# Neighbourhood attention in a hybrid encoder layer: the keys' copies to the other partitions issued by GpSimd in place of SyncE

## The chip, the core and the metric

The kernel runs on one core of a Trainium2 chip. The core has TensorE (PE) for matmuls, VectorE (DVE), ScalarE (ACT) and GpSimd (POOL) for element work, and SyncE (SP), which here does nothing but issue transfers. The transfers themselves are carried by 16 DMA engines that all issuers share. The metric is the time of one launch on the device in microseconds (us). Engines run their own instructions in order and wait for one another through semaphores.

## What is computed

The reference is one layer of an encoder on 512 positions of 1024 channels, in float32: a token mixer, a cross-attention into 256 memory tokens and a gated MLP. The mixer projects the normed input once and feeds three branches, a long convolution (Hyena), a neighbourhood attention and a short gated convolution, whose results are gated and merged. The change lies in the neighbourhood attention. The 512 positions form a grid of 8 rows by 64 columns; each position attends, in each of 8 heads of 64 channels, to all 8 rows and to 16 columns around its own:

```python
s = jnp.einsum('bhrqd,bhrkcd->bhrqkc', qg, k_rows).astype(jnp.float32)
s = s + bias[None].astype(jnp.float32)
s = jnp.where(col_mask[:, None, :], s, -1e30)
p = jax.nn.softmax(s, axis=(-2, -1)).astype(v.dtype)
o = jnp.einsum('bhrqkc,bhrkcd->bhrqd', p, v_rows)
```

## The kernel before

**Split products.** A matmul of the precision needed is made of three: every float32 operand is split into a high part in a shorter format (`high`, ACT, L76) and the remainder (`low`, DVE, L79), and `mm3` (L89 to L91) adds high by high, low by high and high by low in PSUM. A projection (`project`) is eight times `mm3` over tiles of 128 by 512.

**Heads.** The attention works on pairs of heads. `na_project` makes q and k of one pair, 128 channels, by two projections; a head owns 64 of the 128 partitions (`own`), the other half is `oth`. For the scores of a head, q and k are packed so that two matmuls do what three do elsewhere: the tile qa holds the high part of q in `own` and its low part in `oth`; ka holds k's high part in `own` and its low part in `oth`; kb holds the same two parts with the halves exchanged. Then qa by ka (L705) and qa by kb (L706) together give all four products of the parts. A low part is written by DVE straight into the other half of the partitions; the exchange for kb is made by two transfers inside the core, 64 partitions of 512 numbers each (128 KB), the first of the high part (L681), the second of the low part (L682). The second can start only when DVE has written ka's low half. There are 16 such transfers, two for each of 8 heads. kb has three buffers.

**Weights.** `na_weights` (a step: one head and half of its 4 column blocks) needs the bias tiles gm of the head: a transfer on SP loads rpb (L693), and POOL adds the mask to it in three additions (L697), into four buffers that DVE frees when it has added them to the scores (L712). Then softmax. The first step also loads the value tiles v, eight transfers of 256 KB issued by SP (L629).

**What runs beside.** `natten` goes through 19 steps; the four pairs are projected at steps 0, 2, 6 and 10, and a pair that is projected at one of the last three is first used two steps later. In each step one piece of other work is laid between, from a generator (`merge_first`: projections for the merge gates, branch products, and two additions of 128 by 512 on POOL, L803). Their weights are loaded by SP (`load_raw`, L120). Elsewhere POOL also issues transfers: accumulating weight loads before this stage (L106), and loads and stores of factor sums in the MLP (L1096, L1101).

**Order.** The program is written through a layer that derives all semaphores and plans each engine's order when the kernel is built: it takes the instructions by their place in the text, but lets a later one go ahead where the earlier one is not ready by its own reckoning of times. An engine's order is therefore not the text's order, and it is fixed when the kernel runs.

Of the kernel before, what the change touches and what calls it, by code (L numbers as in the profile page):

```python
# [34 lines left out]
def f(ap):  # L35
    return ap.bitcast(F32)
# [10 lines left out]
def shaped(ap, offset, *dims):  # L47

    return bass.AP(ap.tensor, ap.offset + offset, [list(ap.ap[0])] + [list(q) for q in dims])


class Trunk:
# [611 lines left out]
    def na_project(self, pool, hp, x):  # L664

        nc, d = self.nc, self.d
        pq = self.project(d["w_in"][12 + hp], x)
        pk = self.project(d["w_in"][16 + hp], x)
        out = []
        for e in range(2):  # L670
            own, oth = slice(64 * e, 64 * e + 64), slice(64 - 64 * e, 128 - 64 * e)
            qa = pool.tile([P, L], F32R, tag="qa", bufs=4, name="qa")
            src = shaped(pq[own, :], 7 * 64 + 15, [16, 4], [-64, 8], [-1, 16])
            self.high(qa[own, :].rearrange("p (b r c) -> p b r c", b=4, r=8), src)
            self.low(qa[oth, :].rearrange("p (b r c) -> p b r c", b=4, r=8), src,
                     qa[own, :].rearrange("p (b r c) -> p b r c", b=4, r=8))
            ka = pool.tile([P, L], F32R, tag="ka", bufs=4, name="ka")
            kb = pool.tile([P, L], F32R, tag="kb", bufs=3, name="kb")
            self.high(ka[own, :], pk[own, :])
            self.low(ka[oth, :], pk[own, :], ka[own, :])  # L680
            nc.sync.dma_start(out=f(kb[oth, :]), in_=f(ka[own, :]))  # L681
            nc.sync.dma_start(out=f(kb[own, :]), in_=f(ka[oth, :]))  # L682
            out.append([qa, ka, kb, None])
        return out

# [798 lines left out]
```

## Time and profile before

| | us |
|---|---|
| median of three runs | 1085.06 |
| the three runs | 1084.93, 1085.06, 1089.47 |
| the profiled execution | 1087.84 |
| its span, first to last instruction | 1086.1 |
| PE busy in the span | 1056.7 (97%) |
| DVE, ACT, POOL busy | 746.7, 520.1, 101.4 |
| mean granted clock of PE | 0.99 |

The profile is one execution, recorded by the hardware. Its views are a page of totals; waits, that is, who stood idle until whom; the chain of work that ended last, followed backwards; groups of instructions by source line and tile; instructions in order of time; and busy times in chosen stretches, with the granted clock of PE. A tile is named by the program's name. The neighbourhood attention lies between about 240 and 390 us.

### The profile page before, as it was taken

Reading aid. Unit: us, or ns where it says so; the run is one execution under the profiler, and the core shown is the slowest. Engines: PE = TensorE matmul, PEld = TensorE weight load, DVE = VectorE, ACT = ScalarE, POOL = GpSimd, SP = SyncE. Lnnn points to the kernel's source line nnn. Section 1 sums busy time; section 2 is a strip of 40 time slices with the busy share of each in tenths; the row PEclk is TensorE's granted clock in tenths of the full one; section 3 lists DMA queues with packets and bytes.
Section 4 is the critical chain, followed back from the end, with each engine's and each line's share of the span. In section 5 each row is a group of like instructions: output and inputs, shape, how many; then the busy total and the mean of one; then the engine's idle time right before and its main releaser. Section 6 shows DMA issues by size and latency. Waiting matters only on the chain.

```text
span 1086.1 us, 13877 instructions
## 1 busy us (share of the span) xinstructions
PE 1056.7 (97%) x5166; PEld 883.6 (81%) x5166; DVE 746.7 (69%) x1182; ACT 520.1 (48%) x817; POOL 101.4 (9%) x120
## 2 busy tenths in 40 slices
PE   9989999999999999999999999999997999999996
PEld 6768888887888888888798888898886888888885
DVE  7986498874674763436796455579867776667687
ACT  6756554345557642324564444345332434346464
POOL 1061410001120100000000000001211000000000
PEclk9989999999999999999999999999998999999999
DMA  6597986527333322226245321247888333226663
GB/s 226 170 263 204 286 201 159 131 80 181 120 105 94 109 72 97 97 97 232 98 148 195 124 78 43 75 137 271 298 284 275 131 99 112 96 83 193 193 195 126
DMA packets 60400, 167.71 MB, mean 154 GB/s; under 512 B 6473, under 2 KB 13321, under 8 KB 60332
## 3 DMA queue, kind: packets, MB, share of 16 engines
q1 hardware_dynamic: 51116, 133.27, 37.5%
q0 software_dynamic: 9216, 33.56, 11.7%
q8 instruction: 40, 0.66, 0.2%
q14 instruction: 28, 0.23, 0.1%
HBM read 145.83 MB, written 18.87 MB: 152 GB/s over the span
## 4 chain that ended last, share of the span: by engine, by line
PE 76%; DMA 9%; DVE 8%; issue 4%; ACT 2%; POOL 0%; SPq 0%; DVEq 0%; POOLq 0%; ACTq 0%
PE mm L90 23%; PE mm L89 23%; PE mm L91 22%; DMA sums<-sum 4%; DMA sum<-in_ffn_down 2%; PE aux L90 2%; PE aux L89 2%; PE aux L91 2%; DVE wl L79 1%; PE aux L736 1%; PE aux L725 1%; DMA raw<-in_hy_o 1%; DMA nc_raw<-in_xt 1%; DVE hf L431 1%; DMA wr<-in_w_out 0%
## 5 line engine op out<-in xcount | busy, mean ns | idle before, releaser
L79 DVE TENSOR_TENSOR wl<-wr,wh 128x1024 fp32r<-128x1024 f32 (+2 forms) x173 | 209.0, 1210 | 155.9 <-ACT wh L76 155.0
L76 ACT ACTIVATE wh<-wr 128x1024 fp32r<-128x1024 f32 (+3 forms) x193 | 198.2, 1027 | 243.3 <-PE mm L90 174.7
L89 PE MATMUL mm<-hh,wh 128*128 128x512 f32 (+1 forms) x448 | 168.4, 377 | 6.6 <-DVE u L341 6.3
L90 PE MATMUL mm<-hl,wh 128*128 128x512 f32 (+1 forms) x448 | 168.5, 376 | 1.2 <-DVE hl L79 1.2
L91 PE MATMUL mm<-hh,wl 128*128 128x512 f32 (+1 forms) x448 | 168.2, 376 | 0.0
L89 PE MATMUL mm<-xh,wh 128*128 128x512 f32 x416 | 165.0, 397 | 0.0
L90 PE MATMUL mm<-xl,wh 128*128 128x512 f32 x416 | 163.6, 393 | 0.0
L91 PE MATMUL mm<-xh,wl 128*128 128x512 f32 x416 | 163.4, 393 | 0.0
L89 PEld LDWEIGHTS mm<-hh,wh 128*128 128x128 f32 x448 | 84.7, 190 | 22.7 <-issue 7.1
L90 PEld LDWEIGHTS mm<-hl,wh 128*128 128x128 f32 x448 | 84.9, 190 | 16.3 <-DVE hl L79 1.4
L91 PEld LDWEIGHTS mm<-hh,wl 128*128 128x128 f32 x448 | 84.9, 190 | 15.1
L91 PEld LDWEIGHTS mm<-xh,wl 128*128 128x128 f32 x416 | 78.8, 189 | 16.7
L90 PEld LDWEIGHTS mm<-xl,wh 128*128 128x128 f32 x416 | 79.1, 190 | 16.0 <-issue 0.3
L89 PEld LDWEIGHTS mm<-xh,wh 128*128 128x128 f32 x416 | 78.9, 190 | 16.1 <-issue 0.3
L1099 DVE TENSOR_TENSOR sum<-sum 128x512 f32<-128x512 f32 x44 | 30.2, 689 | 24.6 <-DMA sum<-in_ffn_down 24.3
L89 PE MATMUL mm<-wh,sh 128*128 128x512 f32 x110 | 42.8, 389 | 0.0
L91 PE MATMUL mm<-wh,sl 128*128 128x512 f32 x110 | 42.8, 389 | 0.0
L90 PE MATMUL mm<-wl,sh 128*128 128x512 f32 x110 | 42.8, 389 | 0.0
L1035 ACT ACTIVATE u<-u 128x512 f32<-128x512 f32 x22 | 13.9, 632 | 55.2 <-DVE u L341 55.2
L1096 POOL DMA_DIRECT2D sum<-in_ffn_down x22 | 11.8, 536 | 289.2 <-DVE nt L895 234.4
L341 DVE SCALAR_TENSOR_TENSOR u<-mm,cols,u 128x511 f32<-128x511 f32 x44 | 33.0, 749 | 1.0
L333 DVE SCALAR_TENSOR_TENSOR u<-mm,cols,u 128x511 f32<-128x511 f32 x44 | 32.8, 745 | 0.2 <-ACT u L332 0.2
(367 smaller groups left out, 2098.7 us busy)
## 6 DMA issues: line engine op xcount, KB each, us to landing
wr<-in_w_in SPq DMA_DIRECT2D x53, 512.0 KB, 3.5
wr<-in_ffn_up SPq DMA_DIRECT2D x44, 512.0 KB, 4.1
sum<-in_ffn_down POOLq DMA_DIRECT2D x22, 512.0 KB, 4.7
sums<-sum POOLq DMA_DIRECT2D x22, 512.0 KB, 6.2
wl<-in_w_in POOLq DMA_DIRECT2D x20, 512.0 KB, 6.7
wr<-sums SPq DMA_DIRECT2D x20, 512.0 KB, 4.2
wr<-in_ffn_down SPq DMA_DIRECT2D x15, 512.0 KB, 3.5
wr<-in_w_branch SPq DMA_DIRECT2D x12, 512.0 KB, 3.5
```

The lines of the kernel that those rows point to most:

```text
L76: self.nc.scalar.activation(out=out, in_=in_, func=ACT.Copy, bias=0.0, scale=scale)
L79: (eng or self.nc.vector).tensor_tensor(out=out, in0=in_, in1=f(high), op=ALU.subtract)
L89: mm(out, ah, bh, start=first, stop=False)
L90: mm(out, ah, bl, start=False, stop=False)
L91: mm(out, al, bh, start=False, stop=last)
L333: nc.vector.scalar_tensor_tensor(out=out[:, 1:L], in0=ps[:, 0 : L - 1], scalar=self.colvec(w0), in1=out[:, 1:L], op0=ALU.mult, op1=ALU.add)
L341: nc.vector.scalar_tensor_tensor(out=out[:, 0 : L - 1], in0=ps[:, 1:L], scalar=self.colvec(w2), in1=out[:, 0 : L - 1], op0=ALU.mult, op1=A ...
L431: nc.vector.tensor_tensor(out=s, in0=s, in1=part[1][0:1, :], op=ALU.add)
L725: nc.tensor.transpose(tr[:, i * P : (i + 1) * P], s[:, i // 2, (i % 2) * P : (i % 2 + 1) * P], self.ident[:])
L1035: nc.scalar.activation(out=u[:], in_=u[:], func=ACT.Gelu_apprx_tanh)
L1096: nc.gpsimd.dma_start(out=t[:], in_=w[k, i])
L1099: v.tensor_tensor(out=out, in0=x, in1=y, op=ALU.subtract)
```

## The change

The two transfers that fill kb are issued by GpSimd and no longer by SyncE; their data, sizes and dependencies stay as they are.

```diff
             self.high(ka[own, :], pk[own, :])
             self.low(ka[oth, :], pk[own, :], ka[own, :])
-            nc.sync.dma_start(out=f(kb[oth, :]), in_=f(ka[own, :]))
-            nc.sync.dma_start(out=f(kb[own, :]), in_=f(ka[oth, :]))
+            nc.gpsimd.dma_start(out=f(kb[oth, :]), in_=f(ka[own, :]))
+            nc.gpsimd.dma_start(out=f(kb[own, :]), in_=f(ka[oth, :]))
             out.append([qa, ka, kb, None])
         return out
```

## The prediction

> **What bounds the kernel now.** I read the page's busy times first, then TensorE's waits over the whole span, then the chain of waits around the one wait that names the edited tile.
>
> ```profile
> span 1086.1 us, 13877 instructions
> PE 1056.7 (97%) x5166; PEld 883.6 (81%) x5166; DVE 746.7 (69%) x1182; ACT 520.1 (48%) x817; POOL 101.4 (9%) x120
> PE mm L89 <- DVE u L341: 6.3, 2, 6.0
> PE aux L423 <- DVE hf L426: 4.7, 1, 4.7
> PE aux L706 <- DMA kb<-ka: 2.4, 1, 2.4
> PE aux L90 <- DVE sl L79: 1.4, 1, 1.4
> ```
>
> TensorE (PE) sets the time: it is busy for 1056.7 of 1086.1 us, so 29.4 us in all can be won by waiting less. GpSimd (POOL) is nearly idle. The edit can reach PE only through the tile kb, and PE waited for kb once, for 2.4 us (the columns of a wait are total us, times, longest). The chain of waits and PE's instructions in order of time show where:
>
> ```profile
> 251.66 0.69 DVE ka L79
> 252.38 5.30 DMA kb<-ka
> 257.81 0.36 PE aux L706
> ...
> 252.06 0.39 PE L89 MATMUL mm<-xh,wh 128*128 128x512 f32 x1
> 252.40 0.39 PE L705 MATMUL aux<-ka,qa 128*128 128x256 f32 x1
> 252.63 0.39 PE L90 MATMUL mm<-xl,wh 128*128 128x512 f32 x1
> ...
> 255.12 0.28 PE L705 MATMUL aux<-ka,qa 128*128 128x256 f32 x1
> 257.81 0.36 PE L706 MATMUL aux<-kb,qa 128*128 128x256 f32 x1 [2.41 <-DMA kb<-ka]
> ```
>
> This is the first head of the first pair. The second copy of its kb is issued at 252.38, as soon as the low part is written, and lands 5.30 us later at 257.68; PE is free at 255.12 + 0.28 = 255.40 and stands until 257.81. It also shows that PE's order isn't the order of the text: L705 stands among the matmuls of another product, and its partner L706 comes eleven matmuls later. The order is planned when the kernel is built, and a planner that is told of another queue may plan it anew.
>
> The gap is followed by a slow stretch. The columns that matter in the next rows are the stretch, then, after the engines' busy times, the granted clock, the DMA share and GB/s:
>
> ```profile
> 249.00:251.00 2.00, 2.00 (x11) 1.65 (x10) 0.59 (x1) 1.65 (x2) 0.50 (x1) 1.00 1.07 249
> 258.00:259.00 1.00, 1.00 (x7) 0.87 (x7) 0.47 (x1) 0.98 (x2) 0.00 (x0) 0.97 1.06 173
> 259.00:260.00 1.00, 1.00 (x5) 0.80 (x3) 1.00 (x3) 0.45 (x1) 0.00 (x0) 0.50 1.07 198
> 260.00:262.00 2.00, 2.00 (x7) 1.71 (x7) 1.39 (x2) 0.57 (x3) 0.74 (x2) 0.50 0.98 272
> 262.00:264.00 2.00, 2.00 (x9) 1.60 (x9) 1.88 (x4) 0.52 (x3) 1.43 (x2) 0.91 0.81 324
> ```
>
> At half clock PE is "busy" but loses 0.03 + 0.50 + 2 x 0.50 + 2 x 0.09 = 1.71 us of full-speed work. So the one wait costs 2.41 + 1.71 = 4.12 us, and that is the most the edit can win at this place. The shares near 1.0 also say that all DMA engines are saturated there, which is why a copy took 5.3 us.
>
> **The change part by part.** Sixteen copies (two a head) leave SP's queue and enter POOL's. What SP had around the first four, and what the copies cost where nothing else moves:
>
> ```profile
> 251.02 0.52 SPq L681 DMA_DIRECT2D kb<-ka  x1
> 251.59 0.59 SPq L629 DMA_DIRECT2D v<-vd  x1
> 252.38 0.49 SPq L682 DMA_DIRECT2D kb<-ka  x1
> 253.00 0.51 SPq L681 DMA_DIRECT2D kb<-ka  x1
> 253.73 0.46 SPq L682 DMA_DIRECT2D kb<-ka  x1
> 254.28 0.65 SPq L693 DMA_DIRECT2D rpb<-in_na_rpb  x1
> 254.99 0.98 SPq L120 DMA_DIRECT2D wr<-in_w_in  x2
> ...
> kb<-ka SPq DMA_DIRECT2D x4, 128.0 KB, 2.3
> ...
> sum<-in_ffn_down POOLq DMA_DIRECT2D x22, 512.0 KB, 4.7
> wr<-in_ffn_down SPq DMA_DIRECT2D x15, 512.0 KB, 3.5
> ...
> L1096 POOL DMA_DIRECT2D sum<-in_ffn_down x22: 527/532/594, 723.2 to 825.3; - x22
> ```
>
> *Issue.* POOL takes a median of 532 ns for one plain transfer, so sixteen add 16 x 0.53 = 8.5 us to its 101.4; it has the room, and SP gets back about as much (16 x 0.5). The POOL price is measured on 128-partition loads from memory, not on 64-partition copies inside the core; I take it as it is, the copies having fewer rows.
>
> *Landing.* The four copies of the second pair, with the DMA engines less full, landed after 2.3 us, against 5.3 in the first pair: 3.0 us of the first was waiting, behind the value loads (L629) that stand before it in the same queue and beside them on the engines. No row shows this copy issued by POOL. Its bounds: from below 2.3 us, the copy unhindered with POOL no slower than SP; from above 5.3 + 1.2 = 6.5, all the waiting kept, plus the 4.7 - 3.5 = 1.2 us by which POOL's loads of the same matrix landed later than SP's. I take 2.3 + 1.2 for the path, and for the saturated engines the copy's own share counted twice: 128 KB at 249 GB/s is 0.5 us, and shared half and half with SP's transfers it takes 0.5 longer. Together 4.0 us, nearer the lower end, because a copy in POOL's own queue has nothing ahead of it there.
>
> The Trainium skill, DMA: Bandwidth & Descriptors, in its section on SWDGE, HWDGE and iDMA, says that the two kinds of queue are separate inside each DMA engine, which takes them in turn; by that the waiting behind the value loads goes and the sum is the one below. The same page's section "Issuing engines are not separate DMA queues" says that issuing from another engine only saves the issuer's time; by that the 3.0 us stays, which is my first rival. No row of before decides between them.
>
> *The sum.* Landing at 252.38 + 4.0 = 256.38, plus the 0.13 us that passed before from landing to matmul, gives 256.51; PE, free at 255.40, stands 1.1 us in place of 2.41 and wins 1.3. Will the clock still fall? The longest wait that left it whole is this one:
>
> ```profile
> 149.90 0.39 PE L90 MATMUL aux<-sl,wavefh 128*128 128x256 f32 x1 [1.40 <-DVE sl L79]
> ...
> 146.00:150.00 4.00, 2.60 (x13) 1.94 (x11) 4.00 (x8) 3.52 (x4) 1.68 (x2) 1.00 0.76 306
> 150.00:154.00 4.00, 4.00 (x29) 3.78 (x30) 3.97 (x6) 3.71 (x6) 1.28 (x2) 1.00 0.73 124
> ```
>
> After a wait of 1.40 us the clock stayed at 1.00, after 2.41 it halved. A gap of 1.1 lies below the first, so I count the 1.7 us as won: 1.3 + 1.7 = 3.0 us. If PE's order is planned with the copy a little later, other matmuls fill the gap and the win rises towards 4.1; I take no such shift, the lower bound of it. Worth zero is the later end: landing at 6.5 us makes the gap 258.88 + 0.13 - 255.40 = 3.6, a loss of 1.2 and, if the slow stretch doubles, of 2.9.
>
> The Trainium skill, TensorE: Matmul & The Clock Gate, under "Why this matters for your kernels", asks that gaps stay below about 3 us to keep the clock. Here 2.41 us was enough to halve it, so the trace is stricter than the page; by the page's figure the clock would owe nothing to the gap and the win would be 1.3 alone (1083.8).
>
> *The later pairs.* Three more pairs of heads issue four copies each, now behind POOL's additions to the bias tiles (L697), which wait for VectorE:
>
> ```profile
> 280.23 0.50 SPq L682 DMA_DIRECT2D kb<-ka  x1
> 282.80 0.47 SPq L682 DMA_DIRECT2D kb<-ka  x1
> ...
> 278.42 1.44 POOL L697 TENSOR_TENSOR gm<-rpb,mask 128x256 f32<-128x256 f32 x2 [14.95 <-DVE nas L712]
> 285.46 0.74 POOL L697 TENSOR_TENSOR gm<-rpb,mask 128x256 f32<-128x256 f32 x1 [5.61 <-DVE nas L712]
> 289.70 0.76 POOL L697 TENSOR_TENSOR gm<-rpb,mask 128x256 f32<-128x256 f32 x1 [3.49 <-DVE nas L754]
> ...
> 291.11 0.28 PE L706 MATMUL aux<-kb,qa 128*128 128x256 f32 x1
> ```
>
> The second pair's first head needs its kb at 291.11. Issued at 280.23 it lands by 280.23 + 4.0 = 284.2, almost 7 us early; POOL stood idle for 5.61 us before 285.46, room for four issues of 0.53. Even behind the addition at 285.46 (over at 286.20) two issues and 4.0 us end at 291.3, about on time. So I cost the moved queue at nothing, hidden under the matmuls between L681 and L706. In the other direction, additions that come behind copies start up to 2.1 us later, and POOL's own idle time ahead of them (5.61 and 3.49 us) takes that up. SP's loads behind the copies, first the rpb at 254.28 and the weights at 254.99, may go some 2 to 4 us earlier (SP was held from 251.02 on); PE is full there and waits for none of them, so this is worth nothing, though it puts 1 MB more beside the first copies.
>
> The profiled execution took 1087.84 us, 1.74 more than its span and 2.8 more than the median, 1085.06, of the three runs. The sum is made on its stretches and taken off the median: 1085.06 - 3.0 = 1082.0 us.
>
> **The rivals.**
> *No queue of its own* (slower than before). The copies wait on the saturated engines as before and come by POOL's longer path: 6.5 us, gap 3.6. For it: DMA shares of 1.07 on all engines, and the weights that SP now issues earlier. Against it: SP's queue demonstrably held the value load of 251.59 ahead of the copy. It decides as soon as POOL's copy takes over 5.3 us. Time 1085.06 + 1.2 = 1086.3.
> *Caught behind the additions* (slower). If the order on POOL puts a pair's copies behind the addition of 289.70 (over at 290.46), two issues and 4.0 us make 295.5, 4.4 us after 291.11, and 1.7 of slow clock follows: 6.1 us for a pair, 1091.2; 18 for all three, 1103. It decides once copies are issued after about 286. For it: POOL works its queue in order and the additions wait up to 5.6 us; against it: at 280 to 283 POOL stood idle.
> *A new order elsewhere.* The planner moves matmuls or loads beyond this stage. The largest stall is 6.0 us (L89 behind L341); one more such costs 6 before any clock loss and gives 1082.0 + 6 = 1088 or worse, one less 1076. Nothing in the rows says that the order far from the copies should move.
> *Nothing moves*: the copy lands within half a microsecond of 5.3 and the clock falls as before, 1085.
>
> **How the numbers follow.** Forecast, win of 1.3 to 4.1 us: 0.50. No queue of its own: 0.17; nothing moves: 0.08. Caught behind the additions: 0.11. New order: worse 0.09, better 0.05. What a measurement can tell from no change, 0.5%, is 5.4 us, so faster means under 1079.6 and slower over 1090.5. Faster comes from the better new order and a little of the forecast's edge: 0.08. Slower comes from the caught copies and half of the worse order: 0.15. Same: 0.77. The range goes from 1079.5, just beyond the full 4.1 with 1.5 for the spread of the runs, to 1088.5, past the first rival's 2.9 us; left out are the caught copies and the ends of the new order, about 0.2.
>
> **What would show it.** Right: PE's wait at the first L706 is about 1 us or gone, the clock from 258 to 264 stays at 1.00, the first pair's kb lands within about 4 us of its issue, L681 and L682 stand on POOL at some 0.53 us each, no later L706 waits for kb. Wrong: a first landing over 5.3 us, a PE wait for kb in a later pair, POOL issuing those copies after 286, or a new wait of PE over 2 us elsewhere.

## The result, and the profile after

The change made the kernel slower: 1091.45 us against 1085.44 us, medians of 22 runs each, a ratio of 1.0053 with a 95% interval of 1.0039 to 1.0068. That is half a percent, some 5.8 us by the ratio (the medians lie 6.0 apart), where I had forecast 3.0 less.

The page of the changed kernel, and PE's waits over the span (total us, times, longest):

```profile
span 1090.2 us, 13892 instructions
PE 1058.4 (97%) x5166; PEld 885.0 (81%) x5166; DVE 747.3 (69%) x1182; ACT 520.2 (48%) x817; POOL 109.6 (10%) x136
```

```profile
PE aux L706 <- DMA kb<-ka: 5.4, 1, 5.4
PE aux L423 <- DVE hf L426: 4.7, 1, 4.7
PE mm L89 <- DVE u L341: 3.6, 1, 3.6
```

There is still one wait for kb, at the same place, and it grew from 2.4 to 5.4 us. The stage's chain of waits in order of time says why:

```profile
253.41 0.70 DVE ka L79
254.11 0.29 issue
254.40 7.90 DMA kb<-ka
262.30 0.14 issue
262.44 0.55 PE aux L706
```

The second copy, issued by POOL 0.3 us after ka's low half was written, took 7.90 us to land, not 5.30 as before and not 4.0 as I had it. (The whole picture lies 1.75 us later than in the profile of before; that was there ahead of the stage, where the two programs are the same.) SP's queue ahead of the copies, in order of time (start, duration of the issue or of the run of issues), in the kernel before and then in the changed one:

```profile
243.01 4.42 SPq L629 DMA_DIRECT2D v<-vd  x7
251.02 0.52 SPq L681 DMA_DIRECT2D kb<-ka  x1
```

```profile
244.74 5.06 SPq L629 DMA_DIRECT2D v<-vd  x8
250.05 0.62 SPq L693 DMA_DIRECT2D rpb<-in_na_rpb  x1
250.77 2.98 SPq L120 DMA_DIRECT2D wr<-in_w_in  x2
```

Before, rpb and the two weight loads stood behind the four copies, at 254.28 and 254.99. SP had been held by the copies, which waited for ka, ever since the seventh value load was out at 243.01 + 4.42 = 247.43, and not only from 251.02 on, as the prediction has it. Now SP is free: it issues them from 250.05 on, ahead of the copies. That is 192 + 2 x 512 = 1216 KB more on engines that were full before; at the 249 GB/s of before I estimate it at 5.0 us of transfer. The copy did not pay all of that: it landed 2.6 us later than in the profile of before, where the same loads came behind it but were in flight with it. The clock's stretch behind the gap grew with it (the granted clock is the number before the last two):

```profile
260.00:261.00 1.00, 0.00 (x0) 0.00 (x0) 0.00 (x0) 1.00 (x1) 0.00 (x0) 0.61 1.18 188
261.00:262.00 1.00, 0.00 (x0) 0.00 (x0) 0.00 (x0) 0.23 (x1) 0.00 (x0) 0.50 0.62 127
262.00:263.00 1.00, 0.56 (x2) 0.59 (x3) 0.00 (x0) 0.00 (x0) 0.00 (x0) 0.50 0.51 164
263.00:264.00 1.00, 1.00 (x5) 0.90 (x5) 0.47 (x1) 0.00 (x0) 0.00 (x0) 0.50 0.09 33
264.00:266.00 2.00, 2.00 (x8) 1.61 (x7) 2.00 (x4) 0.00 (x0) 0.73 (x1) 0.50 0.00 0
266.00:268.00 2.00, 2.00 (x9) 1.63 (x9) 1.97 (x5) 1.09 (x4) 0.74 (x1) 0.74 0.46 106
```

From PE's restart on, 0.28 + 0.50 + 1.00 + 0.52 = 2.3 us of full-speed work are lost. Gap and clock cost 5.4 + 2.3 = 7.7 us here, against 4.1 in the profile of before. The later pairs cost nothing, as forecast; the second pair's copies on POOL, in order of time:

```profile
283.68 0.74 POOL L697 TENSOR_TENSOR gm<-rpb,mask 128x256 f32<-128x256 f32 x1 [15.72 <-DVE nas L712]
284.36 0.52 POOL L681 DMA_DIRECT2D kb<-ka  x1
284.89 0.76 POOL L697 TENSOR_TENSOR gm<-rpb,mask 128x256 f32<-128x256 f32 x1
285.75 0.53 POOL L682 DMA_DIRECT2D kb<-ka  x1
286.38 0.52 POOL L681 DMA_DIRECT2D kb<-ka  x1
288.33 0.52 POOL L682 DMA_DIRECT2D kb<-ka  x1 [1.43 <-DVE ka L79]
```

They slipped in among the additions, and the transfers of that stretch landed 2.2 us after issue:

```profile
kb<-ka POOLq DMA_DIRECT2D x4, 128.0 KB, 2.2
```

### The profile page after: what moved, and what is told of

The parts are those of the page before. It is cut to its first block, busy times and chain, and to the rows that moved or that the text cites. A ratio compares the mean times of both kernels' runs of the same rounds, so it can differ in the third digit from the quotient of the medians.

```text
span 1090.2 us, 13892 instructions
## 1 busy us (share of the span) xinstructions
PE 1058.4 (97%) x5166; PEld 885.0 (81%) x5166; DVE 747.3 (69%) x1182; ACT 520.2 (48%) x817; POOL 109.6 (10%) x136
## 4 chain that ended last, share of the span: by engine, by line
PE 76%; DMA 8%; DVE 8%; issue 4%; ACT 2%; POOL 1%; SPq 0%; DVEq 0%; POOLq 0%; ACTq 0%
PE mm L89 23%; PE mm L90 23%; PE mm L91 23%; DMA sums<-sum 3%; DMA sum<-in_ffn_down 2%; PE aux L90 1%; PE aux L89 1%; PE aux L91 1%; DVE wl L79 1%; PE aux L736 1%; DMA kb<-ka 1%; PE aux L725 1%; DMA raw<-in_hy_o 1%; DMA nc_raw<-in_xt 1%; POOL sum L1096 1%
## 5 line engine op out<-in xcount | busy, mean ns | idle before, releaser
L89 PE MATMUL mm<-hh,wh 128*128 128x512 f32 (+1 forms) x448 | 169.0, 378 | 3.9 <-DVE u L341 3.6
L89 PE MATMUL mm<-xh,wh 128*128 128x512 f32 x416 | 165.2, 397 | 0.0
L89 PEld LDWEIGHTS mm<-hh,wh 128*128 128x128 f32 x448 | 85.5, 191 | 19.6 <-issue 4.0
L89 PEld LDWEIGHTS mm<-xh,wh 128*128 128x128 f32 x416 | 79.0, 190 | 16.0 <-issue 0.3
L89 PE MATMUL mm<-wh,sh 128*128 128x512 f32 x110 | 42.8, 389 | 0.0
L341 DVE SCALAR_TENSOR_TENSOR u<-mm,cols,u 128x511 f32<-128x511 f32 x44 | 32.9, 748 | 0.9
L712 DVE SCALAR_TENSOR_TENSOR nas<-aux,gm 128x256 f32<-128x256 f32 x32 | 18.1, 608 | 21.7 <-PE aux L706 19.9
```

The source lines that it names most:

```text
L89: mm(out, ah, bh, start=first, stop=False)
L341: nc.vector.scalar_tensor_tensor(out=out[:, 0 : L - 1], in0=ps[:, 1:L], scalar=self.colvec(w2), in1=out[:, 0 : L - 1], op0=ALU.mult, op1=A ...
L712: nc.vector.scalar_tensor_tensor(out=s[:, i, :].rearrange("p (c r) -> p c r", r=8), in0=shaped(ps[:], i * 256, *turned), scalar=0.125, in1 ...
```

## The experiments

Two theories stood after this. **A, the loads let go:** moving the copies frees SP, whose loads get in front of them, and the copies wait for that traffic, whoever issues them. **B, POOL's queue:** a copy issued by POOL is served slower beside SP's queue. Line numbers stay those of the kernel before.

**Only the first pair on POOL, only the later pairs on POOL.** Which copies carry the loss? In the first kernel:

```diff
-            nc.sync.dma_start(out=f(kb[oth, :]), in_=f(ka[own, :]))
+            (nc.sync if hp else nc.gpsimd).dma_start(out=f(kb[oth, :]), in_=f(ka[own, :]))
```

and the same for the second copy; in the second kernel the two engines change places.

> Only the first pair's four copies are issued by POOL, the other twelve by SP. Theory A (loads let go): SP, no longer held by the copies, issues 1.2 MB of rpb and weights ahead of them, and the copies wait for these on the saturated DMA engines. Theory B (POOL's queue): a copy issued by POOL is served slower beside SP's queue, whatever SP issues. Both expect the whole loss here: the first kb lands after about 8 us, PE waits about 5 us at the first L706, time 4 to 7 us over before. If the later pairs carry the loss, landing is as bad but the time is within 2 us of before.

> The complement: the first pair's copies stay on SP, the other twelve go to POOL. Theories A and B both expect the first landing at 5.3 us, PE's wait at 2.4 us, landings of 2 to 3 us in the later pairs and a time within 2 us of before. If POOL's order in the later pairs costs something, 3 us or more over before.

Measured: the first pair alone gives 1.0048 (1.0024 to 1.0073), the whole loss; the later pairs alone 0.9981 (0.9960 to 1.0003), none. PE's wait at the first L706 was 5.30 us in the one and 2.39 us in the other, whose first pair is still SP's. The clock after it, in the second kernel:

```profile
256.34 0.36 PE L706 MATMUL aux<-kb,qa 128*128 128x256 f32 x1 [2.39 <-DMA kb<-ka]
```

```profile
256.00:258.00 2.00, 1.66 (x8) 1.23 (x9) 0.95 (x2) 1.97 (x2) 0.00 (x0) 1.00 1.07 188
258.00:260.00 2.00, 2.00 (x11) 1.74 (x11) 1.93 (x3) 0.04 (x1) 0.21 (x1) 1.00 1.00 264
```

The same wait as before left the clock whole here, so the 1.7 us that I had added to it are not owed each time.

**All copies on POOL, SP held in their place.** Small transfers that read the same halves of ka stand in SP's queue where the copies stood; their target is used by nothing.

```diff
-            nc.sync.dma_start(out=f(kb[oth, :]), in_=f(ka[own, :]))
-            nc.sync.dma_start(out=f(kb[own, :]), in_=f(ka[oth, :]))
+            nc.gpsimd.dma_start(out=f(kb[oth, :]), in_=f(ka[own, :])); nc.sync.dma_start(out=hold[0:1, :], in_=f(ka[own, 0:64])[0:1, :])
+            nc.gpsimd.dma_start(out=f(kb[own, :]), in_=f(ka[oth, :])); self.gone = nc.sync.dma_start(out=hold[1:2, :], in_=f(ka[oth, 0:64])[0:1, :])
```

> All copies on POOL, and in the places of the old copies SP issues transfers of 256 bytes that read the same ka halves, so SP is held as before and its weight loads come behind the copies. Theory A (loads let go): the first kb lands within 5.5 us, PE waits at most 2.5 us, time within 2 us of before. Theory B (POOL's queue): the first kb still lands after about 8 us, PE waits about 5 us, time 4 to 7 us over before.

Measured: 1.0007 (0.9985 to 1.0028), the loss is gone. The profile is less clean than theory A asked: the first landing took 5.93 us and PE waited 3.43.

```profile
251.32 5.93 DMA kb<-ka
257.39 0.55 PE aux L706
```

The weight loads were behind the copies, but rpb was planned ahead of the second one (at 250.99, where SP's first held transfer left room). So the time speaks for A; the landing, and the wait that was to be at most 2.5 us, lie between. A later version pins rpb too.

**All copies on ACT's queue.** The profile of this version lists them as a queue of their own (`q10 hardware_dynamic: 1280, 2.10, 0.8%`, the 16 copies) beside SP's, which has the same kind (`q1 hardware_dynamic`); SP is free as in the change.

```diff
-            nc.sync.dma_start(out=f(kb[oth, :]), in_=f(ka[own, :]))
-            nc.sync.dma_start(out=f(kb[own, :]), in_=f(ka[oth, :]))
+            nc.scalar.dma_start(out=f(kb[oth, :]), in_=f(ka[own, :]))
+            nc.scalar.dma_start(out=f(kb[own, :]), in_=f(ka[oth, :]))
```

> All copies are issued by ACT, whose queue is of the hardware kind like SP's but its own; SP is not held. Theory A (loads let go): as in the change, the first kb lands after about 8 us and PE waits about 5 us. Theory B (POOL's queue): the first kb lands within 5.3 us and PE waits at most 2.4 us. ACT's own order moves too (its copies wait for VectorE), so the total time may differ by 1 to 3 us for that reason; the landing decides.

```profile
251.63 8.00 DMA kb<-ka
259.67 0.58 PE aux L706
```

Measured: 1.0034 (1.0012 to 1.0057), landing after 8.00 us, PE's wait 5.13 us: the change's picture without POOL. So the loss doesn't need POOL; that POOL doesn't bring it by itself is shown by the last version on POOL below.

**Nothing large beside the first copies.** The value loads, and the weight loads of the pieces from step 3 on, are pinned behind the first pair's copies in SP's queue; the values are loaded at step 2.

```diff
-        self.nc.sync.dma_start(out=raw[:], in_=src)
+        with self.tc.issue_after(self.late.ins) if self.late else ExitStack(): self.nc.sync.dma_start(out=raw[:], in_=src)
...
-                self.nc.sync.dma_start(out=t[:], in_=self.vd[:, c : c + 16, :].rearrange("r c x -> c r x"))
+                with self.tc.issue_after(gone): self.nc.sync.dma_start(out=t[:], in_=self.vd[:, c : c + 16, :].rearrange("r c x -> c r x"))
...
-                v = v or self.value_tiles(pool)
+                v = v if step != 2 else self.value_tiles(pool, self.gone.ins); self.late = self.gone if step > 2 else None
```

Here `gone` is the last copy of the first pair. In the second kernel the copies are on POOL and `gone` is the last small transfer that holds SP.

> The copies are on SP as before, and the eight value loads and the two weight loads that compete with the first pair's copies are pinned behind these in SP's queue; nothing large is then in flight beside them. If the traffic in flight is what the copies wait for, the first kb lands within about 2.3 to 3 us of its issue (the later pairs' time), PE's wait at the first L706 is gone or under 0.5 us, and the time is 1 to 4 us below before. If something else makes the first copies slow, they still land after about 5 us and the time stays.

> The same with the copies on POOL; transfers of 256 bytes stand in their places on SP, and the value and weight loads are pinned behind those. Theory A (loads let go) expects the first kb to land as fast as on SP without traffic, within 2.3 to 3 us, PE's wait under 0.5 us and a time within 1.5 us of the version with the copies on SP. Theory B (POOL's queue is slower by itself) expects a landing 1 us or more later than there.

The first pair's copies on SP, then on POOL, in the stretch from 243 to 262 us:

```profile
kb<-ka SPq DMA_DIRECT2D x4, 128.0 KB, 2.3
```

```profile
kb<-ka POOLq DMA_DIRECT2D x4, 128.0 KB, 2.8
```

On SP the copies landed after 2.3 us and PE's list of waits has no kb in it; on POOL after 2.8 us, with a wait of 0.56, a little more than expected. Part of that wait is POOL's order: the second copy was issued at 253.32, behind an addition and the first copy, while SP's small transfer that waited for the same half of ka went out at 252.68. So traffic in flight is what the copies wait for, and POOL's path costs at most half a microsecond here and nothing in the later pairs (2.2). The times are 0.9983 (0.9963 to 1.0003) and 0.9999 (0.9969 to 1.0030): the version on SP may be 2 us better than before, which these runs don't tell from no change.

**The kernels before and after, profiled again.**

> A second profile of the kernel before, to see how far its stretch repeats: both theories expect the first landing at 5.3 us and a wait of 2.4 us, within 0.3 us. Whether the clock halves after the wait is open: it did in the first profile and did not in the version with only the later pairs on POOL, after the same wait.

> A second profile of the changed kernel: both theories expect the first landing near 8 us and a wait of 5.0 to 5.8 us, within 0.5 us of the first profile, with the clock halved behind it.

The wait of PE, of before first and of the changed kernel second:

```profile
257.80 0.36 PE L706 MATMUL aux<-kb,qa 128*128 128x256 f32 x1 [0.62 <-DMA kb<-ka]
```

```profile
257.62 0.55 PE L706 MATMUL aux<-kb,qa 128*128 128x256 f32 x1 [5.33 <-DMA kb<-ka]
```

The changed kernel repeats its wait to 0.05 us. The slow stretch behind its second wait (the wait ends at 257.62):

```profile
258.00:260.00 2.00, 2.00 (x8) 1.71 (x8) 1.28 (x3) 0.00 (x0) 0.59 (x1) 0.50 0.11 39
260.00:262.00 2.00, 2.00 (x8) 1.71 (x7) 2.00 (x3) 0.15 (x1) 0.14 (x1) 0.50 0.00 0
262.00:264.00 2.00, 2.00 (x8) 1.58 (x7) 1.93 (x6) 1.32 (x5) 0.73 (x1) 0.68 0.75 250
```

With 0.2 us of the stretch up to 258 that is 0.2 + 1.0 + 1.0 + 0.64 = 2.8 us lost. The kernel before doesn't repeat itself: its copy landed after 3.54 us this time and PE waited 0.62, with the clock at 1.00.

```profile
254.12 3.54 DMA kb<-ka
```

```profile
258.00:260.00 2.00, 2.00 (x13) 1.74 (x13) 1.49 (x3) 1.97 (x3) 0.00 (x0) 1.00 0.99 248
```

My miss of 1.8 us on this run is the larger lesson: the profile I predicted from showed the worst of three. With the one where only the later pairs moved, before's first pair has waits of 2.41, 2.39 and 0.62 us and one slow stretch of 1.71: on average 1.8 + 0.6 = 2.4 us. The change's first pair (two profiles, and the kernel with the first pair alone) has waits of 5.37, 5.33 and 5.30 and slow stretches that cost 2.3, 2.8 and, worked out in the same way, 3.0: on average 5.3 + 2.7 = 8.0. The difference, 5.6 us, fits the measured 5.8, more closely than three profiles a side can promise: those of before range from 0.6 to 4.1 us. A single execution need not show the loss (these two took 1088.15 us before and 1088.08 after the change, for other stretches vary as much); the medians of many do.

**The loads in front, without POOL; POOL, without the loads in front.** In the first kernel all copies are SP's, but the first head's two are ordered behind the two weight loads; with that order, rpb too goes out ahead of the first pair's copies:

```diff
+def _ahead(self, load):
+    if self.late and self.n < 2:
+        self.n += 1
+        for c in self.first[:2]: self.tc.add_manual_dep(c.ins, load.ins.name, mybir.DependencyInfo(mybir.DependencyClass.NoSync, mybir.DependencyReason.DATA), reason="ahead")
```

(`first` are the copies, `late` is true from step 3 on; the edge is one of order only.) In the second, the version with SP held also pins rpb and the weights behind the small transfers, so that SP's order is that of before.

> All copies on SP, as before, but the first pair's are put behind rpb and the two weight loads in SP's queue: the loads let go, without POOL. Theory A (loads let go) expects the second copy of the first kb to land about as late as in the change, 8 us or more after ka's low half is written, and a time of 2 to 6 us over before (PE's order is planned with the first L706 fourteen matmuls, 3.2 us, later, which hides a part). Theory B (POOL's queue) expects a landing of 5.3 us or less after the issue, no more than 6.5 us after ka's low half, and no wait of PE.

> All copies on POOL, with SP's order exactly as before: 256-byte transfers in the copies' places, rpb and both weight loads behind them. Theory A expects the first landing between 3.5 and 5.5 us, as the two profiles of before have it, and a time within 2 us of before. Theory B expects 7 us or more and a time 4 to 7 us over before. If POOL's queue does get past the value loads, as my prediction had it, the landing is 4 us or less and PE's wait 1 us or less.

> A second profile of the last version, for the spread of its first landing: within 1 us of the first profile if the state of the DMA engines there repeats, up to 2 us apart if it varies as in the two profiles of before (5.3 and 3.5).

SP's order and the chain of the first:

```profile
248.49 0.61 SPq L693 DMA_DIRECT2D rpb<-in_na_rpb  x1
249.21 2.11 SPq L120 DMA_DIRECT2D wr<-in_w_in  x2
251.41 0.52 SPq L681 DMA_DIRECT2D kb<-ka  x1
252.02 0.54 SPq L682 DMA_DIRECT2D kb<-ka  x1
```

```profile
252.02 9.72 DMA kb<-ka
261.88 0.36 PE aux L706
```

SP's order and the chain of the second, where `hold` is the small transfers' target:

```profile
251.55 0.54 SPq L682 DMA_DIRECT2D hold<-ka  x1
253.51 0.66 SPq L693 DMA_DIRECT2D rpb<-in_na_rpb  x1
254.23 1.06 SPq L120 DMA_DIRECT2D wr<-in_w_in  x2
```

```profile
250.84 0.70 DVE ka L79
251.82 3.56 DMA kb<-ka
255.52 0.36 PE aux L706
```

On SP behind the loads the copy landed after 9.72 us and the kernel takes 1.0038 (1.0019 to 1.0057) of before's time, although PE's order now filled part of the gap and the wait itself was 3.24 us. (The profiled execution was the fastest of the twelve, 1086.22 us against a median of 1089.47, and kept its clock; what the others paid here isn't on record.) On POOL with SP's order of before it landed after 3.56 us (3.64 in the second profile, PE waiting 1.03 and 1.14 us), and the time is 0.9987 (0.9960 to 1.0013). For each issuer the result turns with SP's order: theory A holds in both directions. In the first version PE's order moved too, in the second the small transfers came in; these side changes differ, so neither explains both results.

None of the versions is shown to beat the kernel before.

## Why the prediction was wrong

The step that failed is the landing, and in it one sentence: that SP's loads behind the copies "may go some 2 to 4 us earlier", which I called worth nothing "though it puts 1 MB more beside the first copies". The move was there and larger than I had it (rpb from 254.28 to 250.05, with the 1.75 us of offset 6 us earlier, the first weight load as much, the second some 4), because SP was held from 247.43 on; the size was about right. I asked only whether PE waits for those loads, and not what they would do to the copy I was pricing. They were worth, by the estimate above, 5.0 us of transfer in front of a copy whose slack was nothing, and they took its landing from 5.3 us (3.5 in the repeat) to 7.9.

- *Landing 4.0 us, bounds 2.3 to 6.5.* Measured 7.90. The upper bound kept all the waiting of before, but took the traffic of before for granted. With SP's order as it was, POOL's copy landed after 3.56 and 3.64 us and PE waited 1.03 and 1.14, close to the forecast's 4.0 and 1.1: they answer to a kernel that the diff doesn't make. Even there no win is shown, as SP's own copy landed after 3.54 in the repeat of before.
- *A queue of its own has nothing ahead of it.* Only in small part. Behind the same loads, the copy took 9.72 us from issue in SP's own queue, 7.90 in POOL's and 8.00 in ACT's (there the second weight load went out 0.1 us after the copy). A separate queue let the copy past some 1.8 us of that, by one profile in SP's queue, not past the loads. The two sections of the Trainium skill that I weighed (DMA: Bandwidth & Descriptors) come out so: that issuing from another engine is no separate path is nearly what the runs show; taking the queues in turn, as I read it, promised more than they gave.
- *POOL's price.* 16 issues at 0.53 us were forecast; POOL's busy time rose from 101.4 to 109.6, 0.51 each. The 1.2 us for POOL's longer path was too much: the later pairs' copies landed after 2.2 us on POOL and 2.3 on SP, the first pair's without traffic after 2.8 and 2.3.
- *Gap and clock.* The gap was to shrink to 1.1 us and save the clock; it grew to 5.4 and the clock fell in each of the four profiles with a wait over 5 us, for twice as long as in the profile of before. The 4.12 us that I took as the price of the old wait was one profile's; three give 2.4 on average.
- *PE's order.* I took no shift. PE's order in the first pair's stretch changed by one matmul only (an L705 that stood ahead of the waiting L706 now stands behind it), so nothing filled the gap.
- *Later pairs at nothing.* Right: copies among the additions, no PE wait, 0.9981 with these alone. Two copies were issued after 286, which I had named a sign of being wrong, but only because this whole stretch now lies 5.25 us later (the L706 of 291.11 is at 296.36).
- *Rivals.* "No queue of its own" was the nearest case, with the right reason (the weights that SP issues earlier), but priced at 1.2 us from the traffic of before. Caught behind the additions and a new order elsewhere didn't happen.

## What to carry to other kernels

A transfer that waits in an in-order queue also holds back everything behind it, and that may be what keeps a shared resource free for it: before moving it to another queue, list what is behind it, when each of these will now be issued, and whether they meet the moved transfer on the same engines. Price the move with that traffic in front, not with the traffic of the old profile. And before a stall of a few microseconds is worked into a sum, see it in a second profile.

## What was not expected of the hardware

**The clock after a wait is not fixed by the wait's length.** PE waits at the first L706 and the granted clock behind them: 2.39 us, clock 1.00; 2.41, halved; 3.24, 1.00; 3.43, halved; 5.13 to 5.37, halved in all four. Waits elsewhere widen the span: in the version on ACT's queue a wait of 1.97 us at L187 was followed by half clock and one of 3.29 us at L89 was not. The rows of the 3.24 us wait:

```profile
260.00:262.00 2.00, 0.12 (x1) 0.15 (x2) 0.00 (x0) 0.00 (x0) 0.00 (x0) 1.00 0.78 171
262.00:264.00 2.00, 2.00 (x12) 1.78 (x13) 1.37 (x3) 0.00 (x0) 0.70 (x1) 1.00 0.27 96
264.00:266.00 2.00, 2.00 (x11) 1.65 (x10) 1.97 (x4) 1.09 (x4) 0.78 (x2) 1.00 0.00 0
```

What repeats in these waits is how long the clock stays halved. In the profile of before it is twice the 1.71 us lost, 3.4 us. In the changed kernel the rows from 260 on add up to 0.39 / 0.5 + 1 + 1 + 1 + 2 + 2 x 0.26 / 0.5 = 6.8 us, the same stretch twice, and so it is in the other three with a wait over 5 us and in the one of 3.43. It doesn't begin at a fixed point: 1.1 us after PE had gone on in the profile of before, 2.2 us before the end of the wait in the changed kernel.

The Trainium skill, TensorE: Matmul & The Clock Gate (Part 1), describes a window that runs on its own and isn't started by the work; waits near its length would then fall into either state, which is what the four between 2.39 and 3.43 us do.

**What stays open.** Why the second copy of the first kb, in the kernel before, lands after 5.3 us in one execution and 3.5 in another isn't known; the order of its transfers is the same, and no run separates the cause. The 5.93 us of the held version with rpb in front, against 3.56 without, may be rpb's 192 KB or the same spread.
